# Linear attention on one core: working through each 16-head load stage by stage instead of interleaving its groups

## The chip, the cores and the metric

One core of a Trainium2 chip. The metric is device time in microseconds (us), the median of several executions. The profile covers one execution; its span is 1.8 us shorter than the time of the same run (128.9 against 130.71). Engines: TensorE (PE; PEld is its weight load), VectorE (DVE), ScalarE (ACT), GpSimd (POOL) and SyncE (SP). In this kernel GpSimd issues nearly all transfers, and SyncE the first half of the first Q and the last stores. PSUM holds the tiles that the matmuls write (`kva_ps`, `qt_ps` and `o_ps` in the profile). The granted clock is the share of its full speed that TensorE was given, as the profile records it (1.00 or 0.50). In the profile lines, k_raw, q_raw and v_blk are the inputs, kf and qf the features, kva_ps the key-value product, qt_ps the transposed Q features and o_ps the output before the division.

## The reference

```python
def reference(Q, K, V):                       # each 8 x 12 x 512 x 64, float32
    Q_feat = np.maximum(0, Q) + 1
    K_feat = np.maximum(0, K) + 1
    KV = np.einsum('bhkd,bhkv->bhdv', K_feat, V)
    K_sum = np.sum(K_feat, axis=2)
    numerator = np.einsum('bhqd,bhdv->bhqv', Q_feat, KV)
    denominator = np.einsum('bhqd,bhd->bhq', Q_feat, K_sum)
    return numerator / (denominator[:, :, :, None] + 1e-10)
```

## The kernel before

The 96 heads come in 6 loads of 16 heads (`NS = 6`). Each load is two groups of 8 heads (`NG = 12`): load s holds groups 2s and 2s+1. Loads convert float32 to bf16 on the way (K comes as 12 pieces that are 512 KB each in bf16, 6.3 MB in all; the three inputs together are 37.75 MB as read). A group passes through four stages: K features (VectorE), the key-value product (TensorE, copied out by ScalarE), Q features and transposes (VectorE, TensorE, ScalarE), and output (TensorE, then a reciprocal and a multiply on VectorE). The program fixes the order of each engine's work. These parts matter:

```python
    psum_kva = ctx.enter_context(tc.tile_pool(name="psum_kva", bufs=1, space=bass.MemoryType.PSUM))
    psum = ctx.enter_context(tc.tile_pool(name="psum", bufs=2, space=bass.MemoryType.PSUM))
    psum_qt = ctx.enter_context(tc.tile_pool(name="psum_qt", bufs=2, space=bass.MemoryType.PSUM))
    # ...
        for g in range(2, NG - 2):
            k_features(g)
            q_features(g)
            if g > 2:
                transposes(g - 1)
            output(g - 2) if g > 2 else None
            keys_values(g)
            if g % 2:
                s = g // 2
                store(s - 1)
                if s + 2 < NS:
                    load_k(s + 2)
                    load_v(s + 2)
                    load_q(s + 2, parts=2 if s + 2 == NS - 1 else 1)
```

So the output of group g-2 stands between the transposes of g-1 and the product of g. There is one PSUM buffer for the product and two for the transposes. `prepare_v(i)` clears a V buffer once (VectorE and ScalarE share it), `ones_v(i)` puts ones into it.

## Time and profile before

| | before |
|---|---|
| time, median of 3 | 131.71 us (131.33 to 132.43) |
| span of the profile | 128.9 us |
| VectorE, TensorE, ScalarE busy | 50%, 52%, 36% |
| mean granted TensorE clock | 0.87 of full |

Busy shares near 50% say only that no engine is full on average. The chain of waits that ended last, by engine, tells more:

```profile
DMA 52%; DVE 20%; PE 18%; POOL 3%; issue 2%; ACT 2%
```

Over half of the way to the end is a transfer that something waits for. The forty slices of the span and the waits are in the prediction below.

### The profile page before, as it was taken

To read this page: it belongs to the slowest core of one execution; us is meant where nothing else is said; L and a number is where in the kernel's file an instruction comes from. 1 tells how busy PE (TensorE), PEld (TensorE's weight loads), DVE (VectorE), ACT (ScalarE), POOL (GpSimd) and SP (SyncE) were. 2 spreads that over 40 slices of the span, in tenths; PEclk is the share of its full clock that TensorE was granted. 3 is DMA by queue.
4 is the path that set the end of the run, shared out by engine and by line. 5 is a ranking of instruction groups with operands and counts; after the bars stand their busy time and mean duration, and the time that the engine had idled before them with its cause. 6 is when DMAs were issued, how large, how long until landed. Compare 5 with 4: busy or idle time off the path is not lost.

```text
span 128.9 us, 2293 instructions
## 1 busy us (share of the span) xinstructions
PE 66.5 (52%) x960; PEld 46.3 (36%) x960; DVE 64.6 (50%) x151; ACT 47.0 (36%) x76; POOL 26.5 (21%) x45
## 2 busy tenths in 40 slices
PE   0040029786459101978600896900496968755630
PEld 0050016555347001555400564600354745544420
DVE  5862650290395007929004928300965875923970
ACT  7819100822373700063820037450009292079000
POOL 6893222200005600001910000770000200000000
PEclk9999999999999855599996589997569999999555
DMA  4999999999999999999999999999999999999474
GB/s 90 323 205 208 212 201 210 212 209 213 210 212 215 208 248 409 281 205 210 212 217 386 354 201 209 211 215 337 390 227 208 212 210 285 411 362 369 194 311 163
DMA packets 13977, 32.12 MB, mean 249 GB/s; under 512 B 656, under 2 KB 656, under 8 KB 13968
## 3 DMA queue, kind: packets, MB, share of 16 engines
q0 software_dynamic: 11568, 26.74, 92.4%
q1 hardware_dynamic: 2400, 5.24, 10.9%
q8 instruction: 7, 0.11, 0.3%
q14 instruction: 2, 0.02, 0.0%
HBM read 37.75 MB, written 12.58 MB: 390 GB/s over the span
## 4 chain that ended last, share of the span: by engine, by line
DMA 52%; DVE 20%; PE 18%; POOL 3%; issue 2%; ACT 2%
DMA q_raw<-in_Q_dram 39%; DMA k_raw<-in_K_dram 12%; DVE o_sb L199 12%; PE kva_ps L149 11%; DVE v_blk L212 4%; PE qt_ps L173 4%; PE o_ps L188 3%; DVE recip L198 3%; ACT qt L174 2%; POOL k_raw L83 2%; DVE qf L123 1%; POOL v_blk L89 1%; POOL out_dram L115 1%; DVE ones L231 0%
## 5 line engine op out<-in xcount | busy, mean ns | idle before, releaser
L188 PE MATMUL o_ps<-kva_diag,qt 128*64 128x130 bf16 x384 | 20.4, 245 | 35.8 <-DVE o_sb L199 35.4
L149 PE MATMUL kva_ps<-v_blk,kf 64*128 64x320 bf16 x384 | 33.9, 336 | 9.7 <-DMA v_blk<-in_V_dram 8.6
L199 DVE TENSOR_TENSOR o_sb<-o_ps,recip 128x512 f32<-128x512 f32 x48 | 33.2, 691 | 1.6
L159 ACT CAST kva_diag<-kva_ps 64x256 bf16<-64x256 f32 x24 | 8.9, 372 | 66.5 <-PE kva_ps L149 66.2
L174 ACT COPY qt<-qt_ps 128x1024 bf16<-128x1024 bf16 x24 | 29.4, 1301 | 4.9 <-PE qt_ps L173 4.7
L188 PEld LDWEIGHTS <-qt 128*64 128x64 bf16 x384 | 13.6, 120 | 41.9 <-DVE o_sb L199 40.1
L149 PEld LDWEIGHTS <-kf 64*128 64x128 bf16 x384 | 20.7, 106 | 20.4 <-DVE kf L123 9.3
L123 DVE TENSOR_SCALAR qf<-q_raw 128x1024 bf16<-128x1024 bf16 x20 | 7.5, 419 | 30.7 <-DMA q_raw<-in_Q_dram 30.7
L173 PE MATMUL qt_ps<-identity,qf 128*128 128x128 bf16 x192 | 14.2, 232 | 11.9 <-DVE qf L123 9.9
L198 DVE RECIPROCAL recip<-o_ps 128x8 f32<-128x8 f32 x48 | 9.5, 198 | 20.9 <-PE o_ps L188 20.9
L173 PEld LDWEIGHTS <-qf 128*128 128x128 bf16 x192 | 12.0, 104 | 15.1 <-DVE qf L123 10.5
L115 POOL DMA_DIRECT2D out_dram<-o_sb x4 | 3.6, 911 | 64.0 <-DVE o_sb L199 64.0
L123 DVE TENSOR_SCALAR kf<-k_raw 128x1024 bf16<-128x1024 bf16 x24 | 9.0, 418 | 2.8 <-DMA k_raw<-in_K_dram 2.3
L83 POOL DMA_DIRECT2D k_raw<-in_K_dram x12 | 8.1, 677 | 3.9 <-DMA v_blk<-in_V_dram 1.8
L212 DVE MEMSET v_blk<- 128x2925 f32 x3 | 7.5, 2496 | 2.5 <-PEq L299 1.4
L89 POOL DMA_DIRECT2D v_blk<-in_V_dram x12 | 7.5, 635 | 4.7 <-DMA v_blk<-in_V_dram 2.2
L213 ACT COPY v_blk<-zero 128x2195 f32<-128x2195 f32 x3 | 6.0, 2021 | 0.0
L97 POOL DMA_DIRECT2D q_raw<-in_Q_dram x6 | 4.6, 782 | 3.1 <-DMA k_raw<-in_K_dram 3.1
L165 ACT CAST kva_diag<-kva_ps 64x4 bf16<-64x4 f32 x24 | 4.0, 168 | 0.0
L123 DVE TENSOR_SCALAR qf<-q_first 128x1024 bf16<-128x1024 f32 (+1 forms) x4 | 2.1, 564 | 1.7 <-DMA q_first<-in_Q_dram 1.7
L213 ACT ACT_TABLE_LOAD x1 | 1.3, 1283 | 0.7 <-PEq L299 0.7
L228 POOL MEMSET kva_diag<- 128x520 bf16 x3 | 1.5, 558 | 0.0
(10 smaller groups left out, 2.5 us busy)
## 6 DMA issues: line engine op xcount, KB each, us to landing
out_dram<-o_sb POOLq DMA_DIRECT2D x4, 2048.0 KB, 13.9
k_raw<-in_K_dram POOLq DMA_DIRECT2D x12, 512.0 KB, 16.0
v_blk<-in_V_dram POOLq DMA_DIRECT2D x12, 512.0 KB, 19.8
q_raw<-in_Q_dram POOLq DMA_DIRECT2D x4, 1024.0 KB, 25.4
out_dram<-o_sb SPq DMA_DIRECT2D x1, 2048.0 KB, 8.1
out_dram<-o_sb SPq DMA_DIRECT2D x4, 512.0 KB, 2.8
q_first<-in_Q_dram SPq DMA_DIRECT2D x1, 1024.0 KB, 4.9
q_raw<-in_Q_dram POOLq DMA_DIRECT2D x2, 512.0 KB, 24.1
```

The source lines that it names most:

```text
L83: nc.gpsimd.dma_start(out=k_raw[e:P:2], in_=k_dram[e, :, M * s : M * s + M])
L89: nc.gpsimd.dma_start(out=v_blk[s % IN_BUFS][e:P:2, M * e : M * e + M], in_=v_dram[e, :, M * s : M * s + M],)
L123: nc.vector.tensor_scalar(out=dst, in0=src, scalar1=1.0, scalar2=1.0, op0=ALU.add, op1=ALU.max)
L149: nc.tensor.matmul(kva_ps[:, r, 0 : NB * D], lhsT=kf[ps, c, :, :], rhs=vb[ps, :, c, :], start=(c == 0), stop=(c == C2 - 1),)
L159: nc.scalar.copy(out=kva[ps, :, :, n, 0:D], in_=kva_ps[ps, :, 0 : 4 * D].rearrange("p r (e n x) -> p r e n x", e=2, n=2)[:, :, :, n, :],)
L173: nc.tensor.transpose(qt_ps[:, c, :], qf[:, half * C + c, :, :], identity)
L174: nc.scalar.copy(out=qt[:, :, :, half], in_=qt_ps)
L188: nc.tensor.matmul(ops[c // 4][64 * j : 64 * j + 64, c // 2 % 2, (c % 2) * W : (c % 2) * W + W], lhsT=qt[:, c, 32 * b : 32 * b + 32, :], r ...
L198: nc.vector.reciprocal(out=recip, in_=cells[:, :, :, :, D:D1])
L199: nc.vector.tensor_tensor(out=o_sb[:, 2 * (g % 2) + h : 2 * M : 4, 4 * i : 4 * i + 4].rearrange("p n (b c) d -> p b c n d", b=2), in0=cell ...
L212: nc.vector.memset(flat[:, 0:part], 0.0)
L213: nc.scalar.copy(out=flat[:, part:width], in_=zero.to_broadcast([P, width - part]))
```

## The change

The intent: work on both groups of a load as soon as it has landed, with no group held back, so that its store and the next loads can be issued earlier. No instruction is added or removed. The diff, with the removed loop shortened:

```diff
         ones_v(0)
+        ones_v(1)
         q_features(0)
+        transposes(0)
         k_features(0)
-        transposes(0)
+        k_features(1)
         q_features(1)
-        ones_v(1)
+        transposes(1)
         load_k(1)
         load_v(1)
         load_q(1)
+        keys_values(0)
+        keys_values(1)
         prepare_v(2)
         ones_v(2)
         load_k(2)
         load_v(2)
         load_q(2)
-        keys_values(0)
-        k_features(1)
-        transposes(1)
-        output(0)
-        keys_values(1)
-        for g in range(2, NG - 2):
-            ...                      (the loop shown above)
-        a, b = NG - 2, NG - 1
-        ...                          (the last two groups)
+        for s in range(NS):
+            a, b = 2 * s, 2 * s + 1
+            if s:
+                k_features(a)
+                k_features(b)
+                keys_values(a)
+                keys_values(b)
+                q_features(a)
+                transposes(a)
+                q_features(b)
+                transposes(b)
+            output(a)
+            output(b)
+            store(s)
+            if s + 3 < NS:
+                load_k(s + 3)
+                load_v(s + 3)
+                load_q(s + 3, parts=2 if s + 3 == NS - 1 else 1)
```

## The prediction

> **What bounds the kernel now.** I read the page's forty slices first, then the list of waits, then the timeline of each engine, to get the length of every stage.

> ```profile
> PE   0040029786459101978600896900496968755630
> PEclk9999999999999855599996589997569999999555
> DMA  4999999999999999999999999999999999999474
> GB/s 90 323 205 208 212 201 210 212 209 213 210 212 215 208 248 409 281 205 210 212 217 386 354 201 209 211 215 337 390 227 208 212 210 285 411 362 369 194 311 163
> ```

> The DMA row is 9 from the second slice to the 37th (3.22 us each). Loads run at about 210 GB/s (written as bf16), stores near 400. So the kernel is bound by its transfers, and only the last three slices (4, 7, 4) hold idle transfer time. One 16-head load and store take 20.4 us: in the chain of waits the Q of the third load lands at 49.14 and that of the fifth at 90.04, so 40.9 us for two. Those numbers say that computing hurries for nothing today, as long as it takes less than 20.4 us per load. The waits agree:

> ```profile
> POOL out_dram L115 <- DVE o_sb L199: 64.0, 4, 16.8
> ...
> DVE qf L123 <- DMA q_raw<-in_Q_dram: 30.7, 4, 8.8
> ```

> VectorE stood still for Q in four loads, 30.7 us in total, up to 8.8 us each: this is the slack that computing has per load. It is small enough that the question is what the new order makes of one load's latency. The stage lengths are in the timelines of TensorE, then ScalarE, then VectorE:

> ```profile
> 18.57 4.45 PE L149 MATMUL kva_ps<-v_blk,kf 64*128 64x320 bf16 x32 [8.63 <-DMA v_blk<-in_V_dram]
> ...
> 30.46 2.35 PE L149 MATMUL kva_ps<-v_blk,kf 64*128 64x320 bf16 x32 [1.05 <-ACT kva_diag L165]
> ...
> 52.23 3.53 PE L149 MATMUL kva_ps<-v_blk,kf 64*128 64x320 bf16 x32
> ...
> 111.09 2.35 PE L149 MATMUL kva_ps<-v_blk,kf 64*128 64x320 bf16 x32
> 113.37 1.07 PE L173 MATMUL qt_ps<-identity,qf 128*128 128x128 bf16 x16
> 115.80 0.61 PE L173 MATMUL qt_ps<-identity,qf 128*128 128x128 bf16 x8 [1.37 <-ACT qt L174]
> 116.97 0.61 PE L173 MATMUL qt_ps<-identity,qf 128*128 128x128 bf16 x8 [0.56 <-ACT qt L174]
> 117.50 0.64 PE L188 MATMUL o_ps<-kva_diag,qt 128*64 128x130 bf16 x16
> ```

> ```profile
> 114.46 4.79 ACT L174 COPY qt<-qt_ps 128x1024 bf16<-128x1024 bf16 x4
> ```

> ```profile
> 117.96 0.21 DVE L198 RECIPROCAL recip<-o_ps 128x8 f32<-128x8 f32 x1 [4.27 <-PE o_ps L188]
> ...
> 124.15 0.69 DVE L199 TENSOR_TENSOR o_sb<-o_ps,recip 128x512 f32<-128x512 f32 x1
> ```

> The key-value product of one group (32 matmuls) takes 2.35 us at its best, 3.53 after a wait, 4.45 at its first use: the same work at different clocks. The end of the kernel before (from 111 us on) already has the order that the change gives to every load, so it can be measured there: the second product ends at 113.4, and the first output reciprocal comes at 117.96, 4.5 us later, because ScalarE copies 4 kva pieces and then the transposes with only two PSUM buffers; then eight pairs of reciprocal and multiply last to 124.84, 6.9 us.

> [...]every VectorE group stands in the order in which the code emits it[...]. From the windows below, the 0.61 in 44 to 46 us puts a fall at 44.44, and the 0.89 puts another at 119.56[...]. And the half clock stays through the eight output pairs although TensorE is "busy" 1.61 and 1.40 of 2 us there.

> ```profile
> 44.00:46.00 2.00, 0.00 (x0) 0.00 (x0) 0.00 (x0) 0.22 (x1) 0.08 (x1) 0.61 1.13 212
> ...
> 116.00:118.00 2.00, 1.44 (x32) 1.20 (x29) 0.04 (x1) 2.00 (x3) 0.00 (x0) 1.00 1.05 402
> 118.00:120.00 2.00, 0.78 (x18) 0.47 (x14) 1.90 (x6) 1.25 (x2) 0.00 (x0) 0.89 0.58 223
> 120.00:122.00 2.00, 1.61 (x24) 1.03 (x20) 1.93 (x5) 0.00 (x0) 0.00 (x0) 0.50 0.65 257
> 122.00:124.00 2.00, 1.40 (x19) 0.81 (x16) 1.93 (x6) 0.00 (x0) 0.00 (x0) 0.50 0.69 268
> ```

> (The seventh column is the granted clock. It reads 1.00 at 18 to 23 us, where the product took 4.45; I trust the duration there.) [...]

> **The change, part by part.** No instruction is added or removed. In the loop before, a group's product runs between the transposes and outputs of the group before, so the copies of one hide the divisions of another. After, each load is one sequence, and VectorE, TensorE and ScalarE all meet its end.

> *Transfers.* The order on GpSimd's queue is the same (load 1, load 2, store 0, load 3, store 1, ...). Only the issue times move, and there is always a load queued: no gain. The store of load 4, on SyncE's queue, moves with its last output.

> *Start.* V of load 0 lands at 18.5 as before, because the loads ahead of it don't move. First product 18.57 to 23.0, its kva copies to 24.05, second product 24.1 to 26.5, its copies to 27.5. ScalarE's share of preparing the third V buffer (2.02 us) now stands behind these, to 29.5, then the ones on VectorE (0.2). VectorE's output work is queued behind the ones, so the first reciprocal is at 29.7 instead of 24.9; eight pairs later, 29.7 + 6.9 = 36.6, load 1 begins. The V load of load 2 is issued at 29.7 instead of 19, but the queue's earlier loads last to beyond 34: hidden.

> *One load, 1 to 5.* VectorE finishes the load before, then the K features of group a (2 x 0.42 = 0.8); product a 2.35; kva copies a, for there is one kva PSUM buffer (1.05, the wait at 30.46); product b 2.35; 4.5 to the first reciprocal; eight pairs 6.9. Sum 17.95 us with a warm TensorE, every term on the path. Q features and the K features of b lie beside it. But the 12.2 us from the end of product b to the next product a hold the ScalarE-bound transposes and the outputs at half occupancy, which at 119.56 cost the clock in before. So each product a starts at half clock: 4.45 if all of it[...]. [...]I take 4.1 for a and 2.5 for b on average: +1.9, giving 19.85 (17.95 to 22).

> *Sum.* 36.6 + 5 x 19.85 = 135.9 for the last multiply. In before the span ends 4.05 us after it (124.84 to 128.9: last store issued and landed). Span 139.9. The measured median lies 131.71 - 128.9 = 2.8 over the span (the profiled run 1.8): about 142 us, +8%. Does data hold it up further? Q lands at 49, 70, 90, 110, wanted at 57 or later, 77, 97, 117: no. The bound goes from the transfers to the chain of one load's stages, and the queue should run dry near the end: stores of loads 4 and 5 (5.2 us each) can't start before 116 and 130.

> **Rivals.**
> *The clock stays warm.* Then 17.95 per load: 36.6 + 89.8 + 4.05 = 130.4 span, 133 us, +1%. For: in 96 to 118 us the clock held at 1.00 with products and outputs alternating. Against: there every output half-group was followed by a product; the one place with all eight pairs in a row lost the clock and did not get it back.
> *Transfers still bound it and the tail shrinks.* If computing kept up, the early store of load 4 would share the queues with the last load, the last Q would come at 112 to 115, and the end would be 11.2 + 4.05 us later, 127 to 130 span, 129.5 to 132.5 us. For: the 9s in the DMA row and the idle tail. Against: this needs VectorE to be waiting for Q in loads 4 and 5, while my sum has it 6 us late from load 2 on.
> *Worse clock.* If product b also runs cold (2 x 4.45), a load takes 22.1, span 151. For: nothing in the trace after a full product; in 24, 54.7, 75 and 95.6 us the clock came back with the first.

> **Range and chances.** The low end lets the clock come back early or the start be shorter (18.8 a load: 134.7 span, 137 us); the high end lets a load take 20.5 (143.2 span, 145.5). I take 135.5 to 145.5. Slower by over 2% (above 134.3 us): 0.91, the warm rival being the main way out. Within 2%: 0.07. Faster: 0.02.

> **What would show it right or wrong.** Right: VectorE's wait for Q nearly gone; VectorE waiting instead for the K-V products and the transposed copies; each load's K features 19 to 20.5 us after the last; product a near 4 us and product b near 2.4; the DMA row with idle slices from about 115 us; the first output reciprocal at about 30 us. Wrong: product a at 2.35 throughout (warm rival), or VectorE still waiting for Q in the last loads and DMA 9s to the end (transfer rival), or a set that overlaps the next one[...].

Passages that told of the hardware what no trace shows are cut, and each cut is marked. 17.95 us for a load at full clock and 1.9 us for the half clock make 19.85, five of these after 36.6 make 135.9 for the last multiply, 139.9 for the span and about 142 us. 4.1 us for product a and 2.5 for b are the author's estimate between the two durations of the trace, 2.35 and 4.45 us. That an earlier issue gains nothing is the author's estimate too, from the row of 9s in DMA. What VectorE's timeline shows of order is that at the end of before, for one, it runs the outputs from 108.91, the Q features at 112.27 and the next reciprocal at 117.96 us, as the code has them.

## The result, and the profile after

The changed kernel takes 145.04 us (143.72 to 145.36, 4 runs), against 132.07 us (131.33 to 132.45, 4 runs) for the kernel before in the same rounds. The ratio is 1.097, with a 95% interval of 1.088 to 1.106. Ratios here are the mean time of one kernel's fast runs over that of the other's fast runs of the same rounds, so they are not quite the ratio of the medians; medians and ranges are over all runs, slow ones included. Executions over 1.5% slower than the fastest of the same kernel are left out of the means. The span is 143.3 us.

The span of after in forty slices (3.58 us each), busy tenths of TensorE, the granted clock, the transfers, and GB/s:

```profile
PE   0050487355879455776553974775785649794540
PEclk9999999955556975579996599555598555579755
DMA  4999999999999999999999999999999609700274
GB/s 123 285 200 211 211 204 212 211 212 210 211 211 214 344 357 211 212 211 226 406 290 211 212 212 301 399 221 209 211 214 378 249 0 326 264 0 0 117 308 161
```

The transfers have idle slices from the 32nd on: 6, 0, 9, 7, 0, 0, 2. By then the last Q has landed (109.49 us), and the last stores are issued only at 117.68 and from 134.14 us on, when their outputs are computed. TensorE is more busy than before (83.9 us against 66.5) with the same matmuls, which take longer at half clock (a product 4.45 us against 2.35); the mean granted clock is 0.74 against 0.87.

The waits in after (waiting engine and line, what it waited for; us in total, times, longest):

```profile
DVE recip L198 <- PE o_ps L188: 53.8, 5, 12.0
POOL out_dram L115 <- DVE o_sb L199: 46.6, 4, 14.8
...
PE kva_ps L149 <- DVE kf L123: 8.8, 5, 1.9
```

VectorE's wait for Q, 30.7 us before, no longer appears among the waits. In its place VectorE waits five times, once per load, for the first output matmuls, up to 12 us. And before each load TensorE waits for the K features.

The chain of waits that ended last has turned round as well. By engine:

```profile
PE 38%; DVE 28%; ACT 17%; DMA 9%; issue 4%; POOL 0%; ACTq 0%
```

One whole load, the fifth (load 4), in the timelines of TensorE, ScalarE and VectorE (start and length in us, engine, line, operation, count, and in brackets the idle time before it and what ended it):

```profile
98.23 4.45 PE L149 MATMUL kva_ps<-v_blk,kf 64*128 64x320 bf16 x32 [1.71 <-DVE kf L123]
103.67 2.35 PE L149 MATMUL kva_ps<-v_blk,kf 64*128 64x320 bf16 x32 [0.99 <-ACT kva_diag L165]
105.95 1.07 PE L173 MATMUL qt_ps<-identity,qf 128*128 128x128 bf16 x16
108.38 0.61 PE L173 MATMUL qt_ps<-identity,qf 128*128 128x128 bf16 x8 [1.36 <-ACT qt L174]
109.55 0.61 PE L173 MATMUL qt_ps<-identity,qf 128*128 128x128 bf16 x8 [0.56 <-ACT qt L174]
```

```profile
107.04 4.79 ACT L174 COPY qt<-qt_ps 128x1024 bf16<-128x1024 bf16 x4
```

```profile
97.42 1.85 DVE L123 TENSOR_SCALAR kf<-k_raw 128x1024 bf16<-128x1024 bf16 x4
...
110.76 0.21 DVE L198 RECIPROCAL recip<-o_ps 128x8 f32<-128x8 f32 x1 [10.15 <-PE o_ps L188]
...
117.57 1.42 DVE L123 TENSOR_SCALAR kf<-k_raw 128x1024 bf16<-128x1024 bf16 x4
```

Read it as one path: K features at 97.42, the first product from 98.23 to 102.7 at half clock, the second from 103.67 to 106.0 at full clock, transposes that wait for ScalarE's copies, the first reciprocal at 110.76, and the next load's K features at 117.57. That is 20.15 us for this load. The K features of loads 1 to 5 begin at 35.68, 57.27, 77.17, 97.42 and 117.57, and the last multiply ends at 139.23.

The windows of after in which the clock is at half during the outputs (stretch, its length, busy us and instructions of PE, PEld, DVE, ACT and POOL, then clock, DMA share, GB/s):

```profile
76.00:78.00 2.00, 0.07 (x4) 0.03 (x4) 1.97 (x6) 0.00 (x0) 0.46 (x1) 0.50 1.12 210
...
112.00:114.00 2.00, 1.52 (x24) 0.98 (x20) 1.93 (x5) 0.00 (x0) 0.00 (x0) 0.50 0.62 246
114.00:116.00 2.00, 1.45 (x20) 0.80 (x16) 1.93 (x6) 0.00 (x0) 0.00 (x0) 0.50 0.00 0
```

The clock is half when a load's outputs end (0.50 in these windows), and the next load's first product begins at half clock: it took 4.42 to 4.45 us in all five loads.

### The profile page after: what moved, and what is told of

Same layout as the page of the kernel before. It is cut to its first block, busy times and chain, and to the rows that moved or that the text cites. A ratio compares the mean times of both kernels' runs of the same rounds, so it can differ in the third digit from the quotient of the medians.

```text
span 143.3 us, 2296 instructions
## 1 busy us (share of the span) xinstructions
PE 83.9 (59%) x960; PEld 55.2 (39%) x960; DVE 66.5 (46%) x151; ACT 46.7 (33%) x76; POOL 27.3 (19%) x45
## 4 chain that ended last, share of the span: by engine, by line
PE 38%; DVE 28%; ACT 17%; DMA 9%; issue 4%; POOL 0%; ACTq 0%
PE kva_ps L149 30%; DVE o_sb L199 21%; DMA v_blk<-in_V_dram 9%; ACT qt L174 9%; PE qt_ps L173 6%; DVE recip L198 5%; ACT kva_diag L159 4%; ACT v_blk L213 3%; DVE kf L123 3%; PE o_ps L188 2%; ACT L213 1%; ACT kva_diag L165 1%; POOL v_blk L89 0%; DVE v_blk L216 0%; ACTq L159 0%
## 5 line engine op out<-in xcount | busy, mean ns | idle before, releaser
L149 PE MATMUL kva_ps<-v_blk,kf 64*128 64x320 bf16 x384 | 43.2, 400 | 17.5 <-DVE kf L123 8.8
L149 PEld LDWEIGHTS <-kf 64*128 64x128 bf16 x384 | 25.6, 124 | 34.5 <-DVE kf L123 9.9
L188 PE MATMUL o_ps<-kva_diag,qt 128*64 128x130 bf16 x384 | 26.1, 284 | 15.0 <-DVE o_sb L199 12.6
L198 DVE RECIPROCAL recip<-o_ps 128x8 f32<-128x8 f32 x48 | 9.6, 200 | 53.8 <-PE o_ps L188 53.8
L199 DVE TENSOR_TENSOR o_sb<-o_ps,recip 128x512 f32<-128x512 f32 x48 | 33.2, 692 | 1.6
L174 ACT COPY qt<-qt_ps 128x1024 bf16<-128x1024 bf16 x24 | 28.9, 1313 | 6.9 <-PE qt_ps L173 6.8
L173 PE MATMUL qt_ps<-identity,qf 128*128 128x128 bf16 x192 | 15.3, 235 | 21.9 <-DVE qf L123 12.3
L188 PEld LDWEIGHTS <-qt 128*64 128x64 bf16 x384 | 17.0, 142 | 23.6 <-DVE o_sb L199 19.6
L173 PEld LDWEIGHTS <-qf 128*128 128x128 bf16 x192 | 12.6, 106 | 24.7 <-DVE qf L123 12.5
L115 POOL DMA_DIRECT2D out_dram<-o_sb x4 | 3.6, 909 | 46.6 <-DVE o_sb L199 46.6
L123 DVE TENSOR_SCALAR kf<-k_raw 128x1024 bf16<-128x1024 bf16 x24 | 10.4, 496 | 2.5 <-DMA k_raw<-in_K_dram 2.5
L83 POOL DMA_DIRECT2D k_raw<-in_K_dram x12 | 8.6, 721 | 3.9 <-DMA v_blk<-in_V_dram 1.8
L123 DVE TENSOR_SCALAR qf<-q_raw 128x1024 bf16<-128x1024 bf16 x20 | 7.3, 424 | 0.0
L216 DVE COPY v_blk<-ones 128x64 bf16<-128x64 bf16 x3 | 0.5, 196 | 11.4 <-ACT v_blk L213 11.3
L165 ACT CAST kva_diag<-kva_ps 64x4 bf16<-64x4 f32 x24 | 4.0, 168 | 0.0
L123 DVE TENSOR_SCALAR qf<-q_first 128x1024 bf16<-128x1024 f32 (+1 forms) x4 | 2.1, 565 | 0.9 <-DMA q_first<-in_Q_dram 0.9
## 6 DMA issues: line engine op xcount, KB each, us to landing
out_dram<-o_sb POOLq DMA_DIRECT2D x4, 2048.0 KB, 17.2
k_raw<-in_K_dram POOLq DMA_DIRECT2D x12, 512.0 KB, 19.3
```

What stands on the lines that cost most here:

```text
L83: nc.gpsimd.dma_start(out=k_raw[e:P:2], in_=k_dram[e, :, M * s : M * s + M])
L123: nc.vector.tensor_scalar(out=dst, in0=src, scalar1=1.0, scalar2=1.0, op0=ALU.add, op1=ALU.max)
L149: nc.tensor.matmul(kva_ps[:, r, 0 : NB * D], lhsT=kf[ps, c, :, :], rhs=vb[ps, :, c, :], start=(c == 0), stop=(c == C2 - 1),)
L173: nc.tensor.transpose(qt_ps[:, c, :], qf[:, half * C + c, :, :], identity)
L174: nc.scalar.copy(out=qt[:, :, :, half], in_=qt_ps)
L188: nc.tensor.matmul(ops[c // 4][64 * j : 64 * j + 64, c // 2 % 2, (c % 2) * W : (c % 2) * W + W], lhsT=qt[:, c, 32 * b : 32 * b + 32, :], r ...
```

## The experiments

Theory: before waits for its transfers, after for the chain of one load's stages, which is as long as a load's transfers (20.7 against 20.4 us) and contains a product at half clock (4.45 us against 2.35). Rivals: the transfers still set the time, with a worse order or later issues; the new start is what costs; the low clock is only a symptom.

**The new loop behind the old start (e2_new_body).** The start of before up to `keys_values(1)`, then the new loop, with `output(0)` left out because the start has it:

```diff
         (start of before, up to keys_values(1))
         for s in range(NS):
             ...
-            output(a)
+            if s:
+                output(a)
             output(b)
```

> The start of before with the loop of after. Theory (one load's stages in a chain of some 20.7 us, against 20.4 us of transfers): nearly all of the loss stays; only the start is shorter. In before the second product's copies end at 30.4 us, so the outputs of group 1 would run from about 30.9 to 34.3, and load 1 begin at 34.3 instead of 35.7: 1.4 us less than after, about 143.6 us. Rival (the new start is what costs, by delaying the third load's V and the first stores): back to 132 us.

Measured: 142.45 us (141.43 to 143.17, 4 runs), 1.086 times before (1.076 to 1.096). Load 1 begins at 34.17 instead of 35.68 us. Against the 1.097 of after that is 1.5 us less by the ratios, whose intervals overlap. Nearly all of the loss is in the loop.

**The new start with the old loop (e1_new_head).**

```diff
+        (the start of after)
+        output(0)
         for g in range(2, NG - 2):      (the loop of before, unchanged)
```

> The start of after (both groups of load 0 stage by stage, third V buffer prepared behind both products) with the loop of before. Theory: the start's 3 to 4 us are hidden here, because VectorE next needs the Q of load 1, which lands at 34 us, and the transfers already queued last past that: 131 to 132.5 us, like before. Rival (the start has a cost of its own): 134 to 136 us.

Measured: 132.31 us (130.56 to 134.07), 0.998 times before (0.990 to 1.007). Two of its four runs count as slow; the ratio is of the two fast ones (131.25 and 130.56 us). The new start costs nothing measurable with a loop that can catch up. Together with the run above this places the loss in the loop.

**TensorE kept busy with matmuls for nothing (e3_fill_outputs).** All results are right; the extra matmuls write columns of PSUM that nothing reads.

```diff
             for c in range(C):
+                for r in range(4 if c % 4 == 0 else 0):
+                    nc.tensor.matmul(ops[c // 4][:, r % 2, 2 * W : 2 * W + P],
+                                     lhsT=identity, rhs=identity, start=True, stop=True)
         kva_ps = psum_kva.tile([P, 2, BANK], FP32, name="kva_ps")
+        for r in range(16 if g and g % 2 == 0 else 0):
+            nc.tensor.matmul(kva_ps[:, r % 2, NB * D : NB * D + P],
+                             lhsT=identity, rhs=identity, start=True, stop=True)
```

> After, with idle-time matmuls whose results are thrown away: 4 of identity by identity before each output tile, in columns that nothing reads, and 16 ahead of each product a of loads 1 to 5, while TensorE waits for the K features. They should hold the clock up. Theory (half clock at the product is a term of the chain): product a falls from 4.45 to about 2.4 us in five loads and product b from 3.94 to 2.35 in two, 5 x 2.1 + 2 x 1.6 = 13.7 us less: span near 129.6, time 131 to 133 us, with a granted clock above 0.95. If the clock is kept only in some loads, in between. Rival (the order alone, or the transfers, make the loss and the clock is a symptom): 143 to 147 us whatever the clock.

Measured: 136.47 us (135.28 to 137.91), 1.040 times before (1.029 to 1.050), span 135.5. With 272 more matmuls the kernel is 8.6 us faster than after by the medians (145.04 and 136.47, from different rounds) and 7.5 us by the ratios (1.097 and 1.040 of some 131 us). The timeline of TensorE in load 2, the fill first:

```profile
55.39 1.07 PE L147 MATMUL kva_ps<-identity 128*128 128x128 bf16 x16
57.16 2.35 PE L154 MATMUL kva_ps<-v_blk,kf 64*128 64x320 bf16 x32 [0.70 <-DVE kf L123]
60.56 2.35 PE L154 MATMUL kva_ps<-v_blk,kf 64*128 64x320 bf16 x32 [1.05 <-ACT kva_diag L170]
```

Both products take 2.35 us, in all five loads: exactly the 13.7 us that was expected off the products. The time expected was 131 to 133 us, the span 129.6; the span came out at 135.5, so 5.9 of the 13.7 us went again. Load 1 begins at 38.02 instead of 35.68 us: 0.7 us because the very first product ran at half clock throughout in this run (4.45 us, in after 3.69), and 1.6 us because the fill runs at half clock between the output pairs of load 0 (0.61 us for four fill matmuls, 0.40 in load 1). Loads 1 to 4 take 18.3 to 19.1 us and load 5 19.5, instead of 17.95, because a pair takes up to 1.1 us where the fill meets a half clock (from 67.62 to 70.95 us its four matmuls take 0.61 us each time, then 0.40 again). The low clock is a cause here, not a symptom.

**K features of the next load ahead of the outputs (e4_early_features).** Four VectorE instructions per load change place.

```diff
-                k_features(a)
-                k_features(b)
                 keys_values(a)
     ...
+            if s and s + 1 < NS:
+                k_features(a + 2)
+                k_features(b + 2)
             output(a)
             output(b)
     (start)
         keys_values(1)
+        k_features(2)
+        k_features(3)
         prepare_v(2)
```

> After, with only VectorE's K features of the next load moved ahead of the outputs of this one (for load 1 ahead of the third V buffer's preparation). Theory (the chain of one load to the next is the bound): TensorE no longer idles 1.71 to 1.94 us before each product a, so 5 x 1.7 = 8.6 us less, span about 134.7, time about 136.4 us; product a stays near 4.45 us. Rival (transfers set the time): no change, 145 us.

Measured: 132.61 us (131.94 to 132.96), 1.013 times before (1.006 to 1.019), span 130.2. From TensorE's timeline, then the waits, then the transfers' row:

```profile
53.25 3.66 PE L149 MATMUL kva_ps<-v_blk,kf 64*128 64x320 bf16 x32
```

```profile
DVE kf L123 <- DMA k_raw<-in_K_dram: 31.4, 5, 9.7
```

```profile
DMA  4999999999999999999999999999999999995484
```

The gain was 12.4 us by the medians (145.04 and 132.61, from different rounds) and 11.1 by the ratios, where 8.6 was expected. The gap before the product is gone. The output matmuls now run right up to the product, and the clock comes back earlier in it: first products of 3.5 to 4.0 us instead of 4.45. (In load 3 the last output matmuls, 0.65 us from 70.02, reach to the product at 70.60, which took 3.52 us; by an estimate from 3.52, 2.35 and 4.45 some 2.5 us of it were at half clock.) The first products of loads 1 to 4 begin at 35.46, 53.25, 70.60 and 87.76, 17.2 to 17.8 us apart, which is shorter than the transfers of a load, 20.4. From load 2 on VectorE waits three times for the K of the next load, up to 8.7 us and 19.3 us together (the rest of the 31.4 us in the line above falls before load 1), and the transfers are busy to slice 36 again. Here the half clock that is left does no harm, because it no longer makes a load's chain longer than its transfers.

**The third V buffer prepared ahead of the products (e5_early_prepare).**

```diff
+        prepare_v(2)
+        ones_v(2)
         keys_values(0)
         keys_values(1)
-        prepare_v(2)
-        ones_v(2)
```

> After, with the third V buffer prepared before the two products of load 0 as in the kernel before, nothing else. Theory: the first output reciprocal comes at about 26.1 instead of 28.9 us and every later stage with it, 2.8 us less: about 142.2 us. Rival (the start is hidden behind the transfers of loads 1 and 2): 145 us.

Measured: 143.19 us (142.22 to 144.27), 1.094 times before (1.085 to 1.103). In the profile the first reciprocal comes at 26.53 us and load 1 begins at 33.26 instead of 35.68 us, 2.4 us earlier. The lead does not simply pass on to the end: loads 2 to 5 begin 2.2, 1.5, 1.1 and 1.4 us earlier, and the 2.8 us by which the span is shorter (140.5) are reached only in load 5, whose second product ran at full clock this time (2.35 us, in after 3.99). The medians differ by 1.9 us, the ratios by 0.3%, some 0.4 us, and their intervals overlap. So that the earlier start reaches the end is not shown, and neither is its size.

**Fewer loads (e6_after_fewer_loads and e7_before_fewer_loads).** Results wrong (relative error 0.056): K of loads 0 to 2 serves for loads 3 to 5.

```diff
-        k_raw = in_pool.tile([P, M, C2, D], BF16, name="k_raw")
-        for e in range(2):
-            nc.gpsimd.dma_start(out=k_raw[e:P:2], in_=k_dram[e, :, M * s : M * s + M])
+        if s < IN_BUFS:
+            k_all[s] = in_pool.tile([P, M, C2, D], BF16, name="k_raw")
+            for e in range(2):
+                nc.gpsimd.dma_start(out=k_all[s][e:P:2], in_=k_dram[e, :, M * s : M * s + M])
+        k_raw = k_all[s % IN_BUFS]
```

> Wrong on purpose: after without the K loads of loads 3 to 5 (the K of loads 0 to 2 is used again), so 15 us less of transfers (3 x 1.05 MB at 210 GB/s). Theory (the chain of one load's stages is the bound): no gain, 143 to 146 us. Rival (the transfers are still what after waits for): 129 to 133 us.

> Wrong on purpose: before without the same K loads. Theory (before is bound by its transfers, and its interleaved order has up to 8.8 us of slack per load): most of the 15 us shows, 116 to 121 us. Rival (before is bound by computing as well): above 126 us.

Measured: after with fewer loads 145.81 us (143.06 to 146.92). Two of its four runs, the profiled one among them, count as slow; its two fast runs (143.06 and 144.91 us) are 1.098 times before, where after itself was 1.097. In its profile, of a slow run, loads 1 to 5 take 103.2 us together, in after 103.6. Before with fewer loads 121.87 us (120.83 to 123.60), 0.927 times before (0.919 to 0.935). The same 15 us of transfers are worth nothing in after and 9.4 us in before. This is the plainest sign that the bound has moved. Before gave less than all of the 15 us and ended just outside what was expected; where the other 5.6 us went was not followed.

**The end of before, rearranged (e8_tail and e9_tail_again).** Before has a pause near 119 us in which the transfers idle. Two tries to fill it, both with the loop of before:

```diff
(e8)     keys_values(a)                 (e9)     keys_values(a)
-        output(a - 1)                  +        q_features(a)
         keys_values(b)                 +        q_features(b)
-        store(NS - 2)                  +        transposes(a)
         q_features(a)                           output(a - 1)
         transposes(a)                           store(NS - 2)
+        output(a - 1)                           keys_values(b)
+        store(NS - 2)                  -        q_features(a)
         q_features(b)                  -        transposes(a)
                                        -        q_features(b)
         transposes(b)                           transposes(b)
```

> Before with only its last load reordered: both products, then the Q features and transposes of the first of the last two groups, and then the outputs of the group before, so that the last Q, which lands near 109 us, does not wait for those outputs. Theory: the outputs of the last three groups then follow each other without the 4.5 us pause, the transfers' idle time at 119 to 121 us goes, and the end comes 2 to 3 us earlier: 129 to 130 us. Rival (the stores of the last loads set the end): 131 to 132 us.

> A second try at the end of before: the Q features of both last groups and the transposes of the first go ahead of the outputs of the group before, but its key-value product of the last group stays behind them. Estimate from the stage lengths: outputs of group 9 from 110 to 113.2, of group 10 from 115.8, of group 11 to 122.6 instead of 124.85 us: 2.2 us less, 129 to 130 us. Rival (the transfers and the stores of the last two loads set the end, or the outputs of group 9 lose what the others gain): 131 to 133 us.

Measured: e8 132.82 us (132.34 to 133.83), 1.014 times before (1.009 to 1.020), so rather slower. It pulled the Q features forward but held back the outputs of group 9, whose first reciprocal came at 113.34 where before has 108.91. e9 130.92 us (130.19 to 132.25), 0.994 times before (0.987 to 1.000): 0.7 us by the medians, and not clear. Its Q features of group 11 stand ahead of the outputs of group 9 and waited for the second half of Q until 111.08, and its last product then took 3.41 us, where 2.35 is full clock and 4.45 half:

```profile
114.16 3.41 PE L149 MATMUL kva_ps<-v_blk,kf 64*128 64x320 bf16 x32
```

Its last multiply ends at 125.78, no earlier than in before (124.84). Both estimates were wrong in the same way: they moved work into a gap without counting what now stood behind it in the queue.

**Both repairs of after (e10_both_repairs).** The edits of e4 and e5 together.

```diff
+        prepare_v(2)
+        ones_v(2)
         keys_values(0)
         keys_values(1)
+        k_features(2)
+        k_features(3)
-        prepare_v(2)
-        ones_v(2)
     (and the loop of e4_early_features)
```

> After with both small moves: the next load's K features ahead of this load's outputs, and the third V buffer prepared before the products of load 0. Theory: the early features alone already brought the transfers back as the bound (the transfers busy to slice 36, VectorE waiting for K), so the second move gives nothing on top: 131.5 to 133 us. Rival (the chain still has a share, so that an earlier start shows): 1 to 2.8 us less than the early features alone, 130 to 131.5 us.

Measured: 132.70 us (131.08 to 133.55), 1.004 times before (0.996 to 1.012). The earlier start adds nothing clear to the early features. By the ratios (1.004 against 1.013) it gives 1.1 us, the low end of what the rival said, but the intervals overlap, so the rival is not excluded. With the transfers as the bound, the stage-by-stage order is as good as the interleaved one within 2%, and no version clearly beats the kernel before.

## Why the prediction was right

142 us were predicted, with 135.5 to 145.5 as the range, and 145.04 were measured: slower by 9.7% where 8% was said. The mechanism was right; one term was too small, and some luck kept the time inside the range.

*What bounds before.* Right: taking 15 us of transfers away made it 9.4 us faster.

*Transfers don't gain from earlier issues.* Right as far as it was tried. The stores, and the loads behind them, do go out earlier in after (store 0 at 36.06 instead of 39.96 us, store 1 at 57.65 instead of 60.90), V of load 2 goes out later (29.05 instead of 19.00), and the DMA row is 9 up to the 31st slice all the same. The last Q lands at 109.49 us, before at 110.33.

*The start.* 36.6 us was said for load 1; it began at 35.68. The first reciprocal came at 28.88, said 29.7: the first product took 3.69 us instead of 4.45 in this run, since the clock came back within it, at 21.39 us. That is luck: in e3_fill_outputs, e5_early_prepare and e6_after_fewer_loads the same product took 4.45.

*One load.* 19.85 us was said; the five took 21.6, 19.9, 20.2, 20.2 and 21.7 (the fifth to the last multiply), 20.7 on average. The mechanism was right, and the term mis-sized was the half clock. Product a (the first of a load) took 4.42 to 4.45 us in all five loads, where 4.1 was taken. Product b took 3.94, 2.35, 2.35, 2.35 and 3.99, 3.0 on average, where 2.5 was taken; the two long ones:

```profile
41.99 3.94 PE L149 MATMUL kva_ps<-v_blk,kf 64*128 64x320 bf16 x32 [1.05 <-ACT kva_diag L165]
...
123.81 3.99 PE L149 MATMUL kva_ps<-v_blk,kf 64*128 64x320 bf16 x32 [0.99 <-ACT kva_diag L165]
```

Those make 5 x (0.33 + 0.5) = 4.2 us, nearly the whole of the 4.3 us by which the five loads exceeded 5 x 19.85.

The trace shows why. By the trace's clock records the clock changes in after at 21.39, 28.22, 45.29, 52.11, 62.35, 76.01, 82.83, 89.66, 103.31, 110.14, 127.21 and 134.03 us, and any two of these lie a whole multiple of some 3.413 us apart (neighbours by 6.82 to 17.07 us, 2 to 5 times that). The records of before show the same spacing (neighbours by 6.83 to 23.89 us, 2 to 7 times). So cut the span into stretches of 3.413 us on the grid of these records, and read (with `--windows`) how much of a stretch a product filled:

| load | product a in the two stretches that it lies in, us | clock after the second |
|---|---|---|
| 1 | 1.97, 2.48 | stays at half; up at 45.29, after b filled 3.30 |
| 2 | 0.86, 3.41 | up at 62.35 |
| 3 | 1.45, 3.00 | up at 82.83 |
| 4 | 1.67, 2.78 | up at 103.31 |
| 5 | 2.00, 2.44 | stays at half; up at 127.21, after b filled 3.40 |

*The sum.* Load 1 began 0.9 us early, the five loads took 4.3 us more, the end took 4.1 us as said (139.23 to 143.3): 3.4 us more than the predicted span of 139.9. The time missed by 3.0 only, because the step from span to time was 1.8 us where up to 2.8 was taken. The high end of the range let a load take 20.5 us, and 20.7 came: the early first product and that step kept the time just under 145.5.

*How the loss divides.* The landings of Q give it. Before does its last multiply 14.5 us after the last Q has landed (110.33 to 124.84), with the K features of load 5 and the first of its two products already done. After begins load 5 only 8.1 us after that landing (109.49 to 117.57) and then needs 21.7 us. 8.1 + 21.7 - 14.5, less 0.8 for the earlier landing, is 14.4 us before rounding, the growth of the span. The 8 us come from load 1: it begins 1.3 us after its Q (34.43) and takes 21.6 us, but the Q of load 2 lands 15.0 us after that of load 1, with no store issued ahead of it. From then on loads 2 to 4 take 19.9 to 20.25 us and the landings are 19.9 to 20.1 us apart (49.42, 69.52, 89.46, 109.49), so the lateness stays at 7.7 to 8.1 us. (The prediction's own table of landings and starts gave 7 to 8 us; its "6 us late" is a slip.) A chain as long as the transfers cannot make up a lateness. In before VectorE is soon back waiting for the next Q (to 34.21, 49.16, 69.55 and 90.06 us in its timeline).

The half clock sits inside these terms: 5 x 2.1 us for the first products and 1.6 us each for two second ones, 13.7 us. Holding the clock up gave back some 8 us with its own costs in it, and cut the lateness of load 5 to 1.3 us (Q at 110.67, begun at 111.98). e4_early_features caught up entirely: there VectorE is back to waiting, for K.

*The rivals.* The warm rival asked for 1% more and failed because the clock did fall in every load (at 28.22, 52.11, 76.01, 89.66, 110.14 and 134.03 us). The transfer rival failed on e6_after_fewer_loads. The rival with both products cold nearly came true in two of five loads (3.94 and 3.99 us, of 4.45).

What stays open is what makes the clock fall. In after every fall follows a stretch in which TensorE was busy for 1.5 to 1.8 of 3.41 us (before the one at 52.11 us for 1.80, with no pause over 0.8 us), in before the one at 119.54 follows 1.88 us; but in load 2 of after stretches with 1.74 and 1.92 us (65.77 to 72.59) did not lower it.

Two readings need care. In before the first clock record stands at 23.97 us, and the windows from 18 to 24 us read a granted clock of 1.00 while the first product, at 18.57 us, took 4.45 us against 2.35 us later at the same reading; there the durations of equal instructions were taken. And in after four K-feature instructions took 1.84 us in loads 1 to 4, where GpSimd was issuing transfers, and 1.42 us in load 5, where it issued none: 1.3 times. What causes that was not tested.

## What to carry to other kernels

Before you straighten out an interleaved loop, add up the latency of one round with every stage on the path and compare it with the transfers of one round: only what is well below them is free, because what one round falls behind must be caught up in the next (here 20.7 against 20.4 us kept load 5 some 8 us late, and 17.2 to 17.8 us in e4_early_features caught up). If the new order puts a stretch of light TensorE work ahead of a heavy one, price the heavy one at the half clock: here 4.42 to 4.45 us instead of 2.35, in all five loads. And look for the few cheap instructions that the next round needs first: moving four K-feature instructions ahead of the outputs brought back 11 to 12 of the 13 us.
